# Scores of two heads issued one behind the other on the two halves of the array's rows, and stick-breaking sums in two fp32r passes over split data

## The chip, the core and the metric

The kernel runs on one core of a Trainium2 chip. The metric is the device time of one execution in microseconds (us); the time given for a kernel is the median of its runs.

The core's engines work side by side and meet through semaphores: TensorE (PE, with its weight loads, PEld), VectorE (DVE), ScalarE (ACT), GpSimd (POOL) and SyncE (SP), whose queue starts nearly all transfers from HBM. Each engine takes its own instructions in the order in which they stand. Matmuls read SBUF and write PSUM banks.

## The reference

Two blocks on a sequence of 256 tokens of width 1024, batch 1, all in float32. The first block is a Fourier and convolution mixer and a windowed attention, each followed by a mixture of 16 experts. The second has two layers of: half a feed-forward, three attention branches merged by gates, half a feed-forward. The change touches the windowed attention of the first block and two branches of the second. Of these the stick-breaking branch matters most:

```python
def stick_breaking_attention(q, k, v):          # 8 heads of 64
    ...
        z = jnp.einsum('bqhd,bkhd->bhqk', qb, k).astype(jnp.float32) * scale
        strict = kpos[None, :] < qpos[:, None]
        log_one_minus = jnp.where(strict, -jax.nn.softplus(z), 0.0)
        suffix = lax.cumsum(log_one_minus, axis=3, reverse=True) - log_one_minus
        w = jnp.where(strict, jnp.exp(jax.nn.log_sigmoid(z) + suffix), 0.0)
        return jnp.einsum('bhqk,bkhd->bqhd', w.astype(v.dtype), v)
```

So each head needs scores, then a softplus of them, then a running sum of the softplus along the keys, an exponential, and a product with v. The sparse branch (`nsa_attention`) has 8 heads in 2 groups with a compressed, a selected and a windowed part, each a masked softmax; the latent branch (`mla_attention`) has 8 heads with an ordinary causal softmax. The result of each branch goes through a projection and is multiplied by a sigmoid gate:

```python
        y = (gates[:, :, 0] * (o_sb @ proj_sb[l])
             + gates[:, :, 1] * (o_mla @ proj_mla[l])
             + gates[:, :, 2] * (o_nsa @ proj_nsa[l]))
```

## The kernel before

The 256 tokens are two tiles of 128 rows. Large products are done with split operands: a float32 tile w is cast to fp32r by ACT (`wh`, L289) and the remainder is taken by DVE (`wl`, L290); the product is then three fp32r matmuls, hh with wh, hl with wh and hh with wl (L1197 to L1199). Products of the attention itself are plain fp32 matmuls, which the profile shows as two records each.

The kernel is written for a tile framework. It places instructions on the engines by a list of its own: priority goes by the order in which the program is written, an instruction is taken when the framework's own clock says that its inputs are there, and buffers come from tagged pools. PSUM has the pools `mm` (3 banks, for the large products), `at` (2 banks, for scores), `tr` (2, for transposes) and `oa` (1, for outputs). So the order on PE is a mixture: the steps of an attention head, and between them matmuls of whatever later product has its inputs and a bank. In the second block's attention these are the gate product `gates(0)` on the normalised input (`mm<-hh`, `mm<-hl`) and, once a branch's output is there, its projection (`mm<-oh`, `mm<-ol`).

`attention2` issues, per layer: the input products, the stick-breaking branch (`att_sb`, L1454), the compression of the sparse branch, the latent branch (`att_ml`), the gate product, the projection, and the sparse branch (`att_ns`, L1752). In the profiled execution stick-breaking lies at about 1504 to 1565 us (layer 1) and 2189 to 2249 (layer 2), sparse attention at about 1620 to 1673 and 2304 to 2357.

In `att_sb` a head is 64 wide, so two heads share the 128 partitions of a tile: head 2c has rows 0 to 63, head 2c+1 rows 64 to 127. Four pairs c run one after the other. For a pair the scores of both heads are written to two `at` banks (L1462: 256 and 128 columns per head). Then per head: Abs, Exp and Ln on ACT (L1467 to L1469), the softplus `sp` on DVE (L1471, tile `cpT`), two masks on POOL (L1474), the sums as two fp32 matmuls with a triangle of -1 and a block of -1 into the same bank (L1475, 384 columns; L1476, 128 columns), the Exp of the result on ACT (L1479, the tile w, called `ce`), two masks on POOL (L1482), and the product with v (L1436, L1438) into the `oa` bank. A table load on ACT (ACT_TABLE_LOAD) stands where a function is not in the loaded set; Ln, Exp and the Tanh of the gates (L1397) are such functions. The scores of the next pair wait only for their bank, which the Exp of w sets free.

In `att_ns` the scores of two heads on the two halves of the rows are written by L1770 (128 and 256 columns per head), followed by two mask matmuls, a softmax in `causal` (L1290; its maximum of z is L1305), a transpose (L1313) and the product with v (L1782). In the windowed attention `scores` (L694) writes four 256-wide score matmuls per group of two heads (L701), and `heads` (L711) does the softmax.

The constants of the second block, `negT` and `negones` among them, come in one tile `c2` by a DMA that POOL starts before the second block.

## Time and profile before

| | us |
|---|---|
| median of 3 runs | 2604.27 (2604.23 to 2607.89) |
| the profiled execution | 2607.32 |
| its span in the profile | 2605.6 |
| PE busy | 2197.9 (84%) |
| DVE busy | 1171.4 (45%) |
| ACT busy | 884.0 (34%) |
| POOL busy | 90.9 (3%) |
| mean DMA rate | 267 GB/s |

The profile is of one execution. A record's start is exact; the end of a matmul is modelled, so the time that a matmul holds PE is read from its start to the next start. An idle time in brackets stands at the instruction that waited, with the one that released it. Up to about 1222 us the kernel is in the first block, with the DMA engines busy for most of the time, except in the windowed attention (about 640 to 757); behind it lies the second block.

### The profile page before, as it was taken

What the parts mean: (1) busy time and instruction counts of PE and PEld (TensorE: products, weight loads), DVE (VectorE), ACT (ScalarE), POOL (GpSimd) and SP (SyncE); (2) the same over time, 40 slices, a digit from 0 to 9 for tenths busy, and PEclk for the clock granted to TensorE, in tenths of its full rate; (3) what the DMA queues carried; (4) which work ended last, traced back from release to release, by engine and by line L of the source; (5) the groups of instructions that cost most, each with busy time, mean ns of one, the idle gap of its engine ahead of it and who ended that gap; (6) DMA issues with size and microseconds to landing.
All of it is one profiled execution on the core that took longest, in us unless ns stands there. A gap on an engine that the chain in (4) does not pass through costs nothing.

```text
span 2605.6 us, 38741 instructions
## 1 busy us (share of the span) xinstructions
PE 2197.9 (84%) x16264; PEld 1611.9 (62%) x16264; DVE 1171.4 (45%) x2258; ACT 884.0 (34%) x1493; POOL 90.9 (3%) x138
## 2 busy tenths in 40 slices
PE   6977665656977665656999999999999999999999
PEld 4543111113543111113999878799999997879997
DVE  3452110103661101102656657776565556677664
ACT  4331000002441000001544565554444446655443
POOL 1100000000000000000101010000000000000000
PEclk9989878788989878888999999999999999999999
DMA  9779999999759999998455532255555554324553
GB/s 396 321 323 426 428 427 426 427 427 425 296 199 407 427 427 427 427 427 361 176 178 190 178 130 98 84 185 186 179 186 186 178 172 172 114 82 146 180 192 114
DMA packets 67038, 698.82 MB, mean 268 GB/s; under 512 B 7872, under 2 KB 8768, under 8 KB 14256
## 3 DMA queue, kind: packets, MB, share of 16 engines
q1 hardware_dynamic: 66464, 695.38, 67.5%
q8 instruction: 127, 2.08, 0.3%
q0 software_dynamic: 400, 0.98, 0.2%
q14 instruction: 47, 0.39, 0.0%
HBM read 695.28 MB, written 1.05 MB: 267 GB/s over the span
## 4 chain that ended last, share of the span: by engine, by line
PE 50%; ACT 1%; DVE 1%; issue 0%; POOL 0%; ACTq 0%; DVEq 0%
PE mm L1199 11%; PE mm L1198 11%; PE mm L1197 11%; PE mm L1153 1%; PE mm L1154 1%; PE mm L1155 1%; PE at L1770 1%; PE at L1197 1%; PE at L1199 1%; PE at L1198 1%; PE tr L1313 1%; PE oa L1782 1%; PE oa L1436 1%; ACT wh L289 1%; PE at L1475 0%
## 5 line engine op out<-in xcount | busy, mean ns | idle before, releaser
L290 DVE TENSOR_TENSOR wl<-w,wh 128x1024 fp32r<-128x1024 f32 (+3 forms) x494 | 551.5, 1118 | 405.2 <-ACT wh L289 375.9
L289 ACT CAST wh<-w 128x1024 fp32r<-128x1024 f32 (+3 forms) x494 | 472.7, 959 | 597.7 <-PE mm L1198 416.9
L903 PE MATMUL mm<-w,xg 128*32 128x512 f32 x2048 | 322.7, 756 | 210.5 <-DMA w<-in_moe_w_gate_up_dram 209.0
L1198 PE MATMUL mm<-hl,wh 128*128 128x256 f32 x1728 | 490.7, 284 | 2.5 <-DVE hl L1045 2.5
L1199 PE MATMUL mm<-hh,wl 128*128 128x256 f32 x1728 | 491.2, 284 | 0.0
L1197 PE MATMUL mm<-hh,wh 128*128 128x256 f32 x1728 | 491.2, 284 | 0.0
L903 PEld LDWEIGHTS mm<-w,xg 128*32 128x32 f32 x2048 | 65.0, 124 | 436.0 <-DMA w<-in_moe_w_gate_up_dram 321.4
L1198 PEld LDWEIGHTS mm<-hl,wh 128*128 128x128 f32 x1728 | 326.9, 189 | 4.4 <-DVE hl L1045 3.1
L1199 PEld LDWEIGHTS mm<-hh,wl 128*128 128x128 f32 x1728 | 326.7, 189 | 3.7 <-issue 3.4
L1197 PEld LDWEIGHTS mm<-hh,wh 128*128 128x128 f32 x1728 | 326.7, 189 | 0.6 <-issue 0.3
L923 ACT ACTIVATE sil<-mm 128x256 f32<-128x256 f32 x32 | 12.3, 384 | 766.1 <-PE mm L903 766.1
L940 PE MATMUL at<-w,hidT 128*32 128x256 f32 x2048 | 168.7, 485 | 84.7 <-DMA w<-in_moe_w_down_dram 76.9
L924 DVE TENSOR_TENSOR hid<-mm,sil 128x256 f32<-128x256 f32 x32 | 13.6, 425 | 474.1 <-ACT sil L923 474.1
L940 PEld LDWEIGHTS at<-w,hidT 128*32 128x32 f32 x2048 | 78.3, 134 | 163.9 <-DMA w<-in_moe_w_down_dram 73.9
L948 DVE TENSOR_TENSOR xh<-at,agm 32x256 f32<-32x256 f32 x128 | 53.8, 420 | 272.8 <-PE at L940 271.3
L1198 PE MATMUL mm<-gl,wh 128*128 128x256 f32 x528 | 149.3, 283 | 0.0
L1199 PE MATMUL mm<-gh,wl 128*128 128x256 f32 x528 | 148.8, 282 | 0.0
L1197 PE MATMUL mm<-gh,wh 128*128 128x256 f32 x528 | 148.4, 281 | 0.0
L1197 PEld LDWEIGHTS mm<-gh,wh 128*128 128x128 f32 x528 | 99.8, 189 | 0.0
L1199 PEld LDWEIGHTS mm<-gh,wl 128*128 128x128 f32 x528 | 99.6, 189 | 0.0
L1198 PEld LDWEIGHTS mm<-gl,wh 128*128 128x128 f32 x528 | 98.9, 187 | 0.0
L376 PE MATMUL oa<-w,condp 128*32 128x512 f32 x384 | 56.1, 653 | 13.0 <-DMA w<-in_ada_w_dram 12.2
(571 smaller groups left out, 3343.8 us busy)
## 6 DMA issues: line engine op xcount, KB each, us to landing
w<-in_moe_w_gate_up_dram SPq DMA_DIRECT2D x128, 2048.0 KB, 39.1
w<-in_moe_w_down_dram SPq DMA_DIRECT2D x62, 2048.0 KB, 39.1
w<-in_ffn_wi_dram SPq DMA_DIRECT2D x88, 1024.0 KB, 4.8
w<-in_ada_w_dram SPq DMA_DIRECT2D x24, 2048.0 KB, 15.8
w<-in_w_in_dram SPq DMA_DIRECT2D x40, 1024.0 KB, 4.8
w<-in_ffn_wo_dram SPq DMA_DIRECT2D x35, 1024.0 KB, 4.8
w<-in_ffn_wo_dram SPq DMA_DIRECT2D x12, 768.0 KB, 4.4
w<-in_w_out_dram SPq DMA_DIRECT2D x8, 1024.0 KB, 4.8
```

Of the source, the lines that this page charges most:

```text
L289: self.nc.scalar.copy(wh, w)
L290: self.nc.vector.tensor_sub(wl, w, wh.bitcast(F32))
L376: ins = nc.tensor.matmul(ps[32 * j:32 * j + 32, :], self.condp[:, k, 3 - row:35 - row], w[:, k, :], start=first and r == 0, stop=last and ...
L903: nc.tensor.matmul(ps[32 * j:32 * j + 32], xg[:, k, e * CAP:(e + 1) * CAP], w[:, :, kk, j * 256:(j + 1) * 256], start=k == 0, stop=k == KC ...
L940: nc.tensor.matmul(psd[32 * j:32 * j + 32, :], hT2[:, k % 2, 32 * (k // 2):32 * (k // 2) + 32], w[:, kk, j * 256:(j + 1) * 256], start=k = ...
L948: nc.vector.tensor_tensor(dst, psd[32 * j:32 * j + 32, :], gate[32 * j:32 * j + 32, :], op=ALU.mult)
L1153: nc.tensor.matmul(ps[t], xh[:, k, sl], wh[:, c, :], start=k == 0, stop=False)
L1154: nc.tensor.matmul(ps[t], xl[:, k, sl], wh[:, c, :], start=False, stop=False)
L1155: nc.tensor.matmul(ps[t], xh[:, k, sl], wl[:, c, :], start=False, stop=k == kc - 1)
L1197: nc.tensor.matmul(o, wh[:, cs], xh[:, k, :], start=k == 0 and j == 0, stop=False, skip_group_check=True)
L1198: nc.tensor.matmul(o, wh[:, cs], xl[:, k, :], start=False, stop=False, skip_group_check=True)
L1199: nc.tensor.matmul(o, wl[:, cs], xh[:, k, :], start=False, stop=k == kc - 1 and j == 1, skip_group_check=True)
```

## The change

Four things change.

1. In all three places the score matmuls of the two heads get an edge (`queue_behind`) that orders them on PE behind an earlier instruction, without a semaphore: in the windowed attention behind the last step that used the pair of banks (`bank_exp`), in stick-breaking behind the last POOL mask of w of the pair before (`prev`), in sparse attention behind the last maximum of z (`last_exp`). Both heads' scores thus become ready together for the framework's list.
2. The stick-breaking sums: `sp` is split, `sh` by a cast on ACT and `sl` by a subtraction on DVE, and the two fp32 matmuls become four fp32r ones.
3. The constant matrices are copied once to fp32r (`negr`) by two POOL copies.
4. The scratch memory for DMA descriptors made on the core is set to 2048.

```diff
@@ scores(gp, r, bank), windowed attention
-                        nc.tensor.matmul(sps[g][:, t, :], qT[rs, 4 * gp + r, t * P:(t + 1) * P], kT[rs, gp, :],
-                                         start=t == 0, stop=False)
+                        m = nc.tensor.matmul(sps[g][:, t, :], qT[rs, 4 * gp + r, t * P:(t + 1) * P], kT[rs, gp, :],
+                                             start=t == 0, stop=False)
+                        self.queue_behind(m, self.bank_exp.get(bank))
...
-                nc.vector.tensor_tensor(z, z, es, op=ALU.add)
+                self.bank_exp[bank] = nc.vector.tensor_tensor(z, z, es, op=ALU.add)
...
+    def queue_behind(self, ins, prev):
+
+        if prev is not None:
+            self.tc.add_manual_dep(ins.ins, prev.ins.name,
+                                   mybir.DependencyInfo(mybir.DependencyClass.NoSync, mybir.DependencyReason.DATA),
+                                   reason="pair of row tiles")
...
@@ causal
-        nc.vector.tensor_scalar(z, z, 1e-30, None, op0=ALU.max)
+        self.last_exp = nc.vector.tensor_scalar(z, z, 1e-30, None, op0=ALU.max)
...
@@ att_sb
+                prev = None
                 for c in range(4):
...
-                            nc.tensor.matmul(o, SB.kT[r, c, k0:k0 + P], SB.qT[r, c, k0:S], start=k0 == 0, stop=k0 > 0)
+                            m = nc.tensor.matmul(o, SB.kT[r, c, k0:k0 + P], SB.qT[r, c, k0:S], start=k0 == 0, stop=k0 > 0)
+                            self.queue_behind(m, prev)
...
-                        nc.tensor.matmul(z, self.negT, sp, start=False, stop=False, skip_group_check=True)
-                        nc.tensor.matmul(z[:, P:S], self.negones, sp[:, S:S + P], start=False, stop=True,
-                                         skip_group_check=True)
+
+                        sh = self.T(p, [P, 384], "cmh", 2, F32R)
+                        sl = self.T(p, [P, 384], "cml", 2, F32R)
+                        nc.scalar.copy(sh, sp)
+                        nc.vector.tensor_sub(sl, sp, sh.bitcast(F32))
+                        for s_ in (sh, sl):
+                            nc.tensor.matmul(z, self.negr[:, 0:P], s_, start=False, stop=False, skip_group_check=True)
+                            nc.tensor.matmul(z[:, P:S], self.negr[:, P:2 * P], s_[:, S:S + P], start=False,
+                                             stop=s_ is sl, skip_group_check=True)
...
-                            nc.gpsimd.affine_select(s_, s_, [[1, P]], ALU.is_gt, 0.0, 0, -1)
+                            prev = nc.gpsimd.affine_select(s_, s_, [[1, P]], ALU.is_gt, 0.0, 0, -1)
...
@@ att_ns
+                self.last_exp = None
...
-                                    nc.tensor.matmul(sp[g][:, q0:q0 + k1], NS.qT[gs, r, q0:q1], NS.kT[gs, i, 0:k1],
-                                                     start=q0 == 0, stop=False)
+                                    m = nc.tensor.matmul(sp[g][:, q0:q0 + k1], NS.qT[gs, r, q0:q1], NS.kT[gs, i, 0:k1],
+                                                         start=q0 == 0, stop=False)
+                                    self.queue_behind(m, self.last_exp)
...
@@ second_block
+            self.negr = self.T(self.hp, [P, 2 * P], "negr", 1, F32R)
+            nc.gpsimd.tensor_copy(self.negr[:, 0:P], self.negT)
+            nc.gpsimd.tensor_copy(self.negr[:, P:2 * P], self.negones)
...
@@ kernel
-    nc = bacc.Bacc("TRN2", target_bir_lowering=False, num_devices=1)
+    nc = bacc.Bacc("TRN2", target_bir_lowering=False, num_devices=1, dynamic_dma_scratch_size=2048)
```

How this moves work is seen in the order of the instructions on each engine. Line numbers of the kernel after are higher by 10 to 20: its scores are L1473 (stick-breaking) and L1789 (sparse), its sums L1493 and L1494, its casts and subtractions L1490 and L1491, its products with v L1446, L1448 and L1802, its fp32r products L1200 to L1202, its Abs, Exp and Ln L1479 to L1481, its Exp of w L1497.

First, ACT at heads 7 and 8 of layer 1's stick-breaking branch, before. The banks of the two heads are `at_8960` and `at_8961`; L289 are weight casts, L1397 the Tanh of the gates:

```order
L1479 ACT_TABLE_LOAD
L1479 ACTIVATE ce_8976<-at_8960 128x384
L1467 ACTIVATE ce_8980<-at_8961 128x384
L289 CAST wh_9786<-w_9756 128x1024
L1468 ACTIVATE ce_8980<-ce_8980 128x384
L1469 ACT_TABLE_LOAD
L1469 ACTIVATE ce_8980<-ce_8980 128x384
L289 CAST wh_9820<-w_9818 128x1024
L1397 ACT_TABLE_LOAD
L1397 ACTIVATE mg_9530<-mg_9530 128x512
L1479 ACTIVATE ce_8990<-at_8961 128x384
```

And the same heads on ACT after, in the banks `at_8999` and `at_9000`:

```order
L1481 ACT_TABLE_LOAD
L1481 ACTIVATE ce_9005<-ce_9005 128x384
L1490 CAST cmh_9013<-cpT_9009 128x384
L1497 ACT_TABLE_LOAD
L1497 ACTIVATE ce_9021<-at_8999 128x384
L1479 ACTIVATE ce_9025<-at_9000 128x384
L1480 ACTIVATE ce_9025<-ce_9025 128x384
L1481 ACT_TABLE_LOAD
L1481 ACTIVATE ce_9025<-ce_9025 128x384
L1490 CAST cmh_9033<-cpT_9029 128x384
L1497 ACT_TABLE_LOAD
L1497 ACTIVATE ce_9041<-at_9000 128x384
```

The casts have come in, the weight casts and the Tanh have moved ahead of this place, and table loads now stand at Ln and at the Exp of w of both heads.

Second, PE at the same heads before, behind the sums of head 7 (L1475, L1476 on `at_8960`); L1323 and L1324 are the first scores of the latent branch, L1293 and L1294 its masks, and 25 fp32r matmuls stand between this piece and the sums of head 8:

```order
L1475 MATMUL at_8960<-cpT_8970,c_1034_5850 128x384
L1476 MATMUL at_8960<-cpT_8970,c_1034_5850 128x128
L1199 MATMUL mm_9532<-hh_7345,wl_9594 128x256
L1197 MATMUL mm_9532<-hh_7345,wh_9593 128x256
L1198 MATMUL mm_9532<-hl_7346,wh_9593 128x256
L1199 MATMUL mm_9532<-hh_7345,wl_9594 128x256
L1197 MATMUL mm_9531<-hh_7345,wh_9621 128x256
L1323 MATMUL at_9138<-mqk_9136 128x128
L1436 MATMUL oa_8994<-ce_8976,v_8315 64x256
L1324 MATMUL at_9138<-mqk_9136 128x256
```

And after, from the last sum of head 7 to the first product with v of head 8:

```order
L1494 MATMUL at_8999<-cml_9014,negr_5852 128x128
L1333 MATMUL at_9189<-mqk_9187 128x128
L1446 MATMUL oa_9045<-ce_9021,v_8318 64x256
L1334 MATMUL at_9189<-mqk_9187 128x256
L1303 LDWEIGHTS mskb_1667
L1303 MATMUL at_9189<-mskb_1667 128x128
L1304 LDWEIGHTS mskb_1667
L1304 MATMUL at_9189<-mskb_1667 128x128
L1493 MATMUL at_9000<-cmh_9033,negr_5852 128x384
L1494 MATMUL at_9000<-cmh_9033,negr_5852 128x128
L1493 MATMUL at_9000<-cml_9034,negr_5852 128x384
L1494 MATMUL at_9000<-cml_9034,negr_5852 128x128
```

No fp32r product stands between the two heads' sums any more; 18 of them stand ahead of head 7's sums, where 28 stood before.

Third, PE at the scores of one group of sparse attention in layer 1, before (`at_10439` is the bank of one head, the other head's scores follow further down, behind its masks and fp32r products):

```order
L1197 MATMUL mm_10737<-hh_7345,wh_10741 128x256
L1770 MATMUL at_10439<-nkT_9745,qT_9732 128x128
L1770 MATMUL at_10439<-nkT_9745,qT_9732 128x256
L1293 LDWEIGHTS mskb_1667
L1293 MATMUL at_10439<-mskb_1667 128x128
L1294 LDWEIGHTS mskb_1667
L1294 MATMUL at_10439<-mskb_1667 128x128
L1198 MATMUL mm_10737<-hl_7346,wh_10741 128x256
```

And a group after:

```order
L1789 MATMUL at_10439<-nkT_9796,qT_9783 128x128
L1789 MATMUL at_10440<-nkT_9796,qT_9783 128x128
L1789 MATMUL at_10439<-nkT_9796,qT_9783 128x256
L1802 MATMUL oa_10209<-cpT_10398,nkv_8619 64x256
L1802 MATMUL oa_10209<-cpT_10348,nkv_8619 64x128
L1323 MATMUL tr_10416<-cst_72,ce_10407 128x128 x3
L1802 MATMUL oa_10209<-cpT_10398,nkv_8619 64x128
L1802 MATMUL oa_10209<-cpT_10370,nkv_8619 64x256
L1789 MATMUL at_10440<-nkT_9796,qT_9783 128x256
```

The 128-wide scores of the two heads now stand next to each other; between the 256-wide ones other work of the branch has been put.

## Rows read from the trace of the kernel before

**Rows 1.** The page: PE's busy share in forty slices of the span, in tenths.

```profile
PE   6977665656977665656999999999999999999999
```

**Rows 2.** Stretches: us; PE, PEld, DVE, ACT, POOL busy; granted PE clock; DMA share; GB/s.

```profile
640.00:757.00 117.00, 114.01 (x634) 71.98 (x633) 76.74 (x198) 53.93 (x142) 3.12 (x3) 1.00 0.68 266
...
1504.00:1565.00 61.00, 57.85 (x370) 44.88 (x368) 32.63 (x90) 42.89 (x74) 10.05 (x33) 0.97 0.34 121
...
1620.00:1673.00 53.00, 52.91 (x369) 39.29 (x369) 41.00 (x159) 26.92 (x80) 0.00 (x0) 1.00 0.23 81
...
2189.00:2249.00 60.00, 56.88 (x372) 43.62 (x370) 32.84 (x90) 43.16 (x76) 10.43 (x34) 1.00 0.35 123
```

**Rows 3.** Timeline of PE: start, us, engine, line, out<-in, shape; fp32r fill.

```profile
1505.78 0.28 PE L1197 MATMUL mm<-hh,wh 128*128 128x256 f32 x1
1505.90 0.28 PE L1198 MATMUL mm<-hl,wh 128*128 128x256 f32 x1
```

**Rows 4.** Timeline of PE: scores in windowed (L701) and sparse attention (L1770), first mask.

```profile
668.87 0.70 PE L701 MATMUL at<-kT,xn 64*128 64x256 f32 x4
...
674.64 1.13 PE L701 MATMUL at<-kT,xn 64*128 64x256 f32 x4
...
1635.06 0.92 PE L1770 MATMUL at<-nkT,qT 64*128 64x128 f32 x4
1635.91 0.23 PE L1293 MATMUL at<-mskb 128*128 128x128 bf16 x1
```

**Rows 5.** Timeline of PE: the sums of head 7, layer 1, and what follows.

```profile
1552.38 0.91 PE L1475 MATMUL at<-cpT,c 128*128 128x384 f32 x2 [0.72 <-POOL cpT L1474]
1553.13 0.38 PE L1476 MATMUL at<-cpT,c 128*128 128x128 f32 x2
1553.27 0.36 PE L1199 MATMUL mm<-hh,wl 128*128 128x256 f32 x1
```

**Rows 6.** Waits of PE from 1504 to 1565: total us, times, longest.

```profile
PE at L1323 <- ACT ce L1479: 1.3, 1, 1.3
PE at L1475 <- POOL cpT L1474: 0.9, 2, 0.7
```

**Rows 7.** Timeline of ACT at heads 7 and 8 of layer 1.

```profile
1553.60 1.28 ACT L1479 ACT_TABLE_LOAD   x1 [2.47 <-PE at L1476]
1554.89 0.49 ACT L1479 ACTIVATE ce<-at 128x384 f32<-128x384 f32 x1
1555.28 0.48 ACT L1467 ACTIVATE ce<-at 128x384 f32<-128x384 f32 x1
1555.65 1.05 ACT L289 CAST wh<-w 128x1024 fp32r<-128x1024 f32 x1
1556.58 0.54 ACT L1468 ACTIVATE ce<-ce 128x384 f32<-128x384 f32 x1
1557.13 1.28 ACT L1469 ACT_TABLE_LOAD   x1
1558.43 0.52 ACT L1469 ACTIVATE ce<-ce 128x384 f32<-128x384 f32 x1
```

**Rows 8.** Timeline of POOL at the same heads: masks of sp (L1474) and w (L1482).

```profile
1550.71 1.62 POOL L1474 TENSOR_SCALAR_AFFINE_SELECT cpT<-cpT 128x128 f32<-128x128 f32 x2 [4.93 <-DVE cpT L1471]
1555.45 0.54 POOL L1482 TENSOR_SCALAR_AFFINE_SELECT ce<-ce 128x128 f32<-128x128 f32 x2 [3.12 <-ACT ce L1479]
1559.68 0.54 POOL L1474 TENSOR_SCALAR_AFFINE_SELECT cpT<-cpT 128x128 f32<-128x128 f32 x2 [3.70 <-DVE cnb L1299]
```

**Rows 9.** Groups from 1504 to 1565: a cast (ACT) and subtractions (DVE); busy us, mean ns.

```profile
L1287 ACT CAST oh<-oa 128x256 fp32r<-128x256 f32 x3 | 1.1, 370 | 1.9 <-PE oa L1438 1.9
...
L290 DVE TENSOR_TENSOR wl<-w,wh 128x1024 fp32r<-128x1024 f32 x9 | 11.0, 1221 | 3.8 <-ACT wh L289 2.4 <-PE mm L1199 1.3
L1288 DVE TENSOR_TENSOR ol<-oa,oh 128x256 fp32r<-128x256 f32 x3 | 1.3, 425 | 3.6 <-ACT oh L1287 3.5
```

**Rows 10.** Stretch with a lower granted clock, columns as in rows 2.

```profile
1558.00:1561.00 3.00, 3.00 (x17) 3.00 (x16) 2.26 (x4) 0.94 (x2) 0.54 (x2) 0.55 0.31 57
```

More of the change, by code (lines that the diff above doesn't have):

```diff
@@ L706, in scores, with heads @@
                 return sps
-            def heads(gp, r, sps):
+            self.bank_exp = {}
+            def heads(gp, r, sps, bank):
                 h0 = 8 * gp + r
@@ L762, in windowed @@
                     next(q1, None)
-                heads(0, r, sc)
+                heads(0, r, sc, self.at)
                 if r < 3:
@@ L770, in windowed @@
                 nx = scores(1, r + 1, self.mm if r % 2 == 0 else self.at) if r < 3 else None
-                heads(1, r, sc)
+                heads(1, r, sc, self.mm if r % 2 else self.at)
                 sc = nx
```

## The prediction

> **What bounds the kernel now.** I read the page's slices first, then the table by stage, then the lines and waits of TensorE (PE), and last the timelines of ScalarE (ACT) and GpSimd (POOL). In the page's line of forty slices PE stands at 9 from about the twentieth on [rows 1]. So in the second block, time is PE work plus PE's idle time, and no other engine counts unless PE waits for it. The table by stage says the same where the change lies: of 53.0 us of sparse attention in layer 1 PE is busy 52.9; of 61.0 us of stick-breaking it is busy 57.9 in layer 1, and 56.9 of 60.0 in layer 2 [rows 2]. The windowed stage of the first block is PE-bound too (114.0 of 117.0 us) [rows 2], though what surrounds it there is not. The idle 3.1 us of a stick-breaking stretch have names: 1.3 us for the Exp of w and 0.9 us for the POOL selects [rows 6]; the rest is a copy behind a table load.
>
> PE keeps busy there because the scheduler fills between the heads' steps with split-precision fp32r matmuls of the gate projection, each 256 columns wide and 0.12 us behind the one before (1505.78, 1505.90) [rows 3]. A head's own steps are a long chain on other engines; the fill is what hides it. That is the view to keep in mind below: the change makes PE's part shorter and the chain longer.
>
> **The change part by part: the PE stream.** *Scores.* Two heads whose row tiles stand next to each other run together: four records take 0.70 us paired and 1.13 us unpaired in the windowed stage [rows 4], so a full pair of 256-wide ones saves 0.43 us and a 128-wide one beside a wider one about half, 0.22. Sparse attention has no pair before: one head's four records hold PE 0.85 us (1635.06 to 1635.91) [rows 4]. The order shows how many become neighbours per layer: in sparse attention 5 pairs of 128, 1 of 256 and 2 mixed, of 16 possible, because transposes and output products are put between the others; in stick-breaking 3 mixed ones beyond those that stood together before. That is 5 x 0.22 + 0.43 + 2 x 0.22 + 3 x 0.22 = 2.6 us per layer. In the windowed stage 12 pairs stand together for 10, 2 x 0.43 = 0.85 us once.
>
> *Sums.* A head's two fp32 sums hold PE 0.89 us, from 1552.38 to 1553.27 [rows 5]. After, there are four fp32r matmuls, two of 384 and two of 128 columns. By the 256-wide step [rows 3] a 384-wide one is an estimated 0.18 us. No 128-wide fp32r stands in the trace: its price lies between half of the 256-wide step, 0.06, and the 0.22 that the 128-wide fp32 sum holds PE: 0.14 to the next start (1553.13 to 1553.27) and the 0.08 by which that next one is longer [rows 3, 5]; I take the whole 256-wide step, 0.12, as nearest in form. Then 2 x 0.18 + 2 x 0.12 + 0.1 for entering = 0.70, a gain of 0.19 a head, 1.5 us per layer (0 to 2.5).
>
> *Switches.* The first fp32r matmul after an fp32 one takes 0.36 instead of 0.28 us (1553.27 against 1505.78) [rows 3, 5], so a change of form costs about 0.09. Counted in the two orders, the attention stretch of a layer has 286 changes of form before and 266 after, so 1.8 us less. The Trainium skill ("TensorEngine Tiling (Array Packing)", Key Properties) says that changing the tiling mode drains TensorE; it would speak against more row-tile groups, and the 0.09 is what rows show of it. Since groups become fewer it counts for the change here.
>
> Stream: -2.6 - 1.5 - 1.8 = -5.9 us per layer (-3.5 to -7.5).
>
> **The chain.** Per head the change adds an ACT cast and a VectorE (DVE) subtraction between the POOL selects and the sums. Casts of 256 and 1024 columns take 0.37 and 1.05 us, subtractions 0.43 and 1.22 [rows 7, 9]; for 384 that is by the line 0.48 and 0.56. And the scores of the next pair now stand behind the last POOL select of this pair, where before each head's scores went out as its bank came free. ACT's order, shown above, adds a second thing: per layer 12 instead of 8 table loads in the stretch, since Ln and Exp of the last heads now each have their own. A load holds ACT 1.30 us (1557.13 to 1558.43) [rows 7]. The Trainium skill ("ScalarE: Activation LUTs", What ACT_TABLE_LOAD costs) puts 1.28 us plus a drain of 1.38 on each switch; the rows show no such drain, as the load starts when the Exp ahead of it ends. By the skill's price four loads of the last pair would cost some 5 us more per layer than I count.
>
> The last pair (heads 7 and 8 of a layer) in after's order, from the end of its scores, by rows [rows 7 to 9]: Abs 0.37, Exp 0.55, load 1.30, from Ln's start to the end of the selects 1.79 (1558.43 to 1560.22), cast 0.48, subtraction 0.56, sums of the low half 0.4, load 1.29 (it waits for the sums, as at 1553.60), Exp of w 0.39: 7.1 us. Head 8's Abs stands behind that Exp on ACT, so head 8 goes through the same again, and ends with 1.10 from Exp's start to the selects' end (1554.89 to 1555.99) instead of 0.39: 7.8 us. Together 15.0. In that time PE has in its order 18 fp32r matmuls (2.2 us), the sums (1.4) and one score group of the next branch with its output products (some 1.3): 4.9. PE then sits idle **10 us**, where before 28, 5 and 25 fp32r matmuls stood at these places and 2.2 us were waited for [rows 6]. The fill has been used up: it was put between the earlier heads, and what remains of it needs this branch's output.
>
> The third pair has 74 fp32r matmuls (8.9 us), sums and small work, 11.8 us in all, against a chain of the same 15 to 16 us: 4 us idle at most. Pairs one and two have 72 and 82 of them and the fp32 compression matmuls, 13 to 14 us against 13 to 16. Since fill and chain are near each other there I take 3 us for the three together, not the 6 of the upper ends. So 13.0 instead of 3.1 idle: **+9.9 us per layer** (+4 to +14).
>
> *Clock.* After the wait at 1553.60 the granted clock stood at 0.55 in 1558 to 1561, near the lower of the two levels; 17 matmuls took 3.0 us where 17 x 0.12 = 2.0 would do [rows 10]. Layer 2's stretch has no such clock (1.00) [rows 2]. With longer waits I count one more, +1.0 (0 to 3).
>
> *The rest costs nothing.* The two POOL copies of the constants run in the norm ahead of the second block's first matmuls, where POOL is idle. The smaller DMA scratch leaves the 460 instructions of SyncE's queue and POOL's DMAs in the same order; if it did delay a POOL DMA, the transfers of the first block are bound by weights, not by it. In sparse attention the edge puts scores behind an earlier head's z maximum on DVE. No head there has a table load, a cast or a POOL select in its chain, PE waits 0.1 us in 53 now [rows 2], and fill from the projections still stands between the heads; if that cover went, eight groups with 0.5 us each would cost 4 us a layer, which the range holds.
>
> **The sum.** Per layer -5.9 + 9.9 = +4.0; two layers +8.0; windowed -0.85; clock +1.0: +8.2 us. On the profiled execution (2607.3 us, of it 2605.6 span) this gives 2615.5. That execution was 3.0 above the median of 2604.3, which I take as spread between runs, so 2612.5, rounded **2612**.
>
> **The rivals.** *The fill still hides the chain* (faster). Then idle time stays at 3.1 us and the stream's gain comes through: 2 x -5.9 - 0.85 = -12.7, 2591.6. For it: PE's fill of pairs one to three is hardly smaller than before, and the casts are short. Against it: 18 matmuls stand before the last pair's sums and none between head 7's and head 8's. It decides where idle time grows by under 3.7 us a layer, since -5.9 + 3.7 doubled is -4.4, with the windowed stage -5.2. Chance 0.14. *Both cancel*: the last pair idles 7 us instead of 10 and the others stay covered, +6 against -5.9: 2604, chance 0.23. *The pairs do not run together*: the two halves share more than the windowed stage shows, the scores' 2.6 and 0.85 are lost: 8.2 + 6.05 = +14.2, 2618, chance 0.05. *Everything small is dear*: 128-wide fp32r at 0.22, selects at the 1.6 us seen once, idle +13, a half-clock stretch in each layer: 2 x (-4.5 + 13) - 0.85 + 3 = +19, 2623, chance 0.08. The forecast, 2606 to 2618, has 0.50.
>
> **How the numbers follow.** A measurement of this kernel can tell 0.2%, 5.2 us, from no change: 2599.1 to 2609.5 counts as same. Slower: 0.43 of the forecast's 0.50, and 0.13 of the last two, 0.56, and 0.02 from the upper edge of the cancelling case: 0.58. Same: 0.07 of the forecast, 0.17 of the cancelling case, 0.02 of the first rival: 0.26. Faster: 0.12 of the first rival and 0.04 of the cancelling case's lower edge: 0.16. The range 2596 to 2624 leaves out most of the first rival and a little above the last.
>
> **What would show it.** In the profile of after: idle time of PE in each stick-breaking stretch (57.9 of 61.0 now) grows to about 13 us, most of it at the sums and output products of heads 7 and 8, waiting for casts, subtractions and the Exp of w behind table loads; 12 table loads there; sums of 0.70 us a head; pairs of scores that start together; sparse attention shorter by 1 to 3 us with no wait; perhaps stretches of clock near 0.5. The prediction is wrong if PE's idle time there stays under 7 us, if the sums' fp32r passes cost as fp32, or if time moves in a stage that is not attention.

## The result: 30 us slower, where 8 were forecast

The changed kernel takes 2635.9 us (median of 4 runs, 2633.5 to 2637.8) against 2606.1 for the kernel before in the same runs (2604.2 to 2608.0): a ratio of 1.0115, 95% interval 1.0099 to 1.0131. The forecast was 2612, in a range of 2596 to 2624. The sign was right; the size was not.

The span grew from 2605.6 to 2633.6 us, by 28.0. From the first starts of the scores' lines in the two traces: the windowed attention takes 6.6 us of it (the first stick-breaking scores start at 1510.9 for 1504.3), layer 1 takes 9.8 (from one layer's first scores to the next layer's 694.8 for 685.0), and layer 2 the last 11.6. No other stage moved by more than 0.3 us.

These are the stretches of the changed kernel, columns as in [rows 2]: the windowed stage, stick-breaking in layer 1, sparse attention in layer 1, stick-breaking in layer 2, and the last pair of heads of layer 1 by itself. The first line is of the kernel before, for the windowed stage.

```profile
669.00:735.00 66.00, 63.01 (x396) 34.44 (x396) 45.13 (x134) 30.79 (x102) 2.08 (x2) 1.00 0.65 251
669.00:742.00 73.00, 68.45 (x403) 35.04 (x401) 45.18 (x134) 30.81 (x102) 2.08 (x2) 0.95 0.63 243
1511.00:1582.00 71.00, 60.55 (x405) 48.43 (x405) 37.78 (x101) 54.24 (x92) 10.86 (x34) 0.92 0.34 119
1641.00:1700.00 59.00, 57.13 (x408) 41.87 (x408) 44.53 (x149) 30.23 (x80) 0.00 (x0) 1.00 0.22 76
2206.00:2277.00 71.00, 60.18 (x406) 48.02 (x405) 37.99 (x102) 54.17 (x92) 10.85 (x34) 0.93 0.33 119
1568.00:1584.00 16.00, 9.73 (x34) 6.34 (x33) 4.23 (x12) 9.49 (x17) 2.15 (x8) 0.58 0.00 0
```

Two columns matter. PE idles 10.5 us of a stick-breaking stretch (71.00 less 60.55), where [rows 2] had 3.1. And the granted clock is 0.92 and 0.93 over a whole stretch, 0.58 in the last pair, where before one stretch of layer 1 alone was low [rows 10]. The waits of PE from 1511 to 1582 answer to [rows 6] (total us, times, longest):

```profile
PE at L1493 <- ACT cmh L1490: 5.6, 4, 2.3
PE oa L1446 <- POOL ce L1500: 2.6, 4, 0.9
PE tr L1677 <- issue: 0.9, 1, 0.9
PE at L1333 <- ACT ce L1497: 0.6, 1, 0.6
```

The sums wait for the new cast, the output products for the masks of w, and a score for the Exp of w. The chain that the prediction walked through shows on ACT (timeline, answering to [rows 7]) at heads 7 and 8:

```profile
1565.98 0.49 ACT L1479 ACTIVATE ce<-at 128x384 f32<-128x384 f32 x1 [0.33 <-PE at L1473]
1566.51 0.53 ACT L1480 ACTIVATE ce<-ce 128x384 f32<-128x384 f32 x1
1567.05 1.28 ACT L1481 ACT_TABLE_LOAD   x1
1568.34 0.52 ACT L1481 ACTIVATE ce<-ce 128x384 f32<-128x384 f32 x1
1570.09 0.51 ACT L1490 CAST cmh<-cpT 128x384 fp32r<-128x384 f32 x1 [1.23 <-POOL cpT L1486]
1570.62 1.28 ACT L1497 ACT_TABLE_LOAD   x1
1572.08 0.49 ACT L1497 ACTIVATE ce<-at 128x384 f32<-128x384 f32 x1 [0.18 <-PE at L1494]
1572.47 0.48 ACT L1479 ACTIVATE ce<-at 128x384 f32<-128x384 f32 x1
...
1577.26 0.51 ACT L1490 CAST cmh<-cpT 128x384 fp32r<-128x384 f32 x1 [1.92 <-DVE cnb L1309]
1577.79 1.28 ACT L1497 ACT_TABLE_LOAD   x1
1579.25 0.49 ACT L1497 ACTIVATE ce<-at 128x384 f32<-128x384 f32 x1 [0.18 <-PE at L1494]
```

From Abs of head 7 at 1565.98 to the output product of head 8 at 1580.15 are 14.2 us; the walk had 15.0. (The load for the Exp of w starts ahead of the sums here, not behind them as at 1553.60 in [rows 7], which saves time; the sums, at half the clock, take some of it back.) On PE the same time looks like this; the waits stand in brackets:

```profile
1567.86 0.28 PE L1200 MATMUL mm<-oh,wh 128*128 128x256 f32 x1
...
1570.66 0.68 PE L1493 MATMUL at<-cmh,negr 128*128 128x384 f32 x1 [2.29 <-ACT cmh L1490]
1571.13 0.31 PE L1494 MATMUL at<-cmh,negr 128*128 128x128 f32 x1
...
1572.62 0.79 PE L1333 MATMUL at<-mqk 96*128 96x128 f32 x2 [0.58 <-ACT ce L1497]
...
1577.82 0.69 PE L1493 MATMUL at<-cmh,negr 128*128 128x384 f32 x1 [1.99 <-ACT cmh L1490]
...
1580.15 0.69 PE L1446 MATMUL oa<-ce,v 128*64 128x256 f32 x1 [0.94 <-POOL ce L1500]
```

Also to be seen: the 384-wide sum lasts 0.68 us here, and 0.34 to 0.45 in the heads before, at full clock. From 1570.7, just behind the wait of 2.29 us, the granted clock was at half, and the little work that PE had ran at half speed. PE idles 5.8 us of these 14.2, where the walk had 10 of 15.

### The profile page after: what moved, and what is told of

It is laid out like the page before. It is cut to its first block, busy times and chain, and to the rows that moved or that the text cites. A ratio compares the mean times of both kernels' runs of the same rounds, so it can differ in the third digit from the quotient of the medians.

```text
span 2633.6 us, 38778 instructions
## 1 busy us (share of the span) xinstructions
PE 2200.0 (84%) x16264; PEld 1606.9 (61%) x16264; DVE 1182.9 (45%) x2274; ACT 902.1 (34%) x1517; POOL 91.3 (3%) x140
## 4 chain that ended last, share of the span: by engine, by line
PE 48%; ACT 2%; DVE 2%; issue 1%; POOL 0%; ACTq 0%; DVEq 0%; POOLq 0%
PE mm L1201 11%; PE mm L1200 11%; PE mm L1202 11%; PE mm L1156 1%; PE mm L1158 1%; PE mm L1157 1%; DVE wl L290 1%; PE at L1200 1%; PE at L1789 1%; PE at L1201 1%; PE at L1202 1%; PE tr L1323 1%; PE oa L1802 1%; PE oa L1446 1%; ACT wh L289 1%
## 5 line engine op out<-in xcount | busy, mean ns | idle before, releaser
L289 ACT CAST wh<-w 128x1024 fp32r<-128x1024 f32 (+3 forms) x494 | 472.6, 959 | 581.7 <-PE mm L1201 402.3
L1200 PE MATMUL mm<-hh,wh 128*128 128x256 f32 x1728 | 490.9, 284 | 0.0
L1202 PE MATMUL mm<-hh,wl 128*128 128x256 f32 x1728 | 489.3, 283 | 0.0
L1200 PEld LDWEIGHTS mm<-hh,wh 128*128 128x128 f32 x1728 | 325.9, 189 | 4.4 <-issue 4.1
L1202 PEld LDWEIGHTS mm<-hh,wl 128*128 128x128 f32 x1728 | 326.0, 189 | 1.3 <-issue 1.1
L927 DVE TENSOR_TENSOR hid<-mm,sil 128x256 f32<-128x256 f32 x32 | 13.6, 424 | 490.1 <-ACT sil L926 490.1
L943 PE MATMUL at<-w,hidT 128*32 128x256 f32 x2048 | 163.4, 473 | 78.0 <-DMA w<-in_moe_w_down_dram 69.2
L1202 PE MATMUL mm<-gh,wl 128*128 128x256 f32 x528 | 148.8, 282 | 0.0
L1200 PE MATMUL mm<-gh,wh 128*128 128x256 f32 x528 | 148.5, 281 | 0.0
L1200 PEld LDWEIGHTS mm<-gh,wh 128*128 128x128 f32 x528 | 99.9, 189 | 0.0
L1202 PEld LDWEIGHTS mm<-gh,wl 128*128 128x128 f32 x528 | 99.5, 189 | 0.0
L376 PE MATMUL oa<-w,condp 128*32 128x512 f32 x384 | 58.6, 665 | 13.0 <-DMA w<-in_ada_w_dram 12.0
```

The source lines that it names most:

```text
L289: self.nc.scalar.copy(wh, w)
L376: ins = nc.tensor.matmul(ps[32 * j:32 * j + 32, :], self.condp[:, k, 3 - row:35 - row], w[:, k, :], start=first and r == 0, stop=last and ...
L943: nc.tensor.matmul(psd[32 * j:32 * j + 32, :], hT2[:, k % 2, 32 * (k // 2):32 * (k // 2) + 32], w[:, kk, j * 256:(j + 1) * 256], start=k = ...
L1200: nc.tensor.matmul(o, wh[:, cs], xh[:, k, :], start=k == 0 and j == 0, stop=False, skip_group_check=True)
L1202: nc.tensor.matmul(o, wl[:, cs], xh[:, k, :], start=False, stop=k == kc - 1 and j == 1, skip_group_check=True)
```

## Where the layers' time went, by line

Since every matmul's start is exact, the time from each start to the next, less idle time, can be added up by line. This was done for layer 2, from its first scores to the first matmul of the feed-forward behind the attention. This is the hold of a line; the hold of all lines together is the stream. The three kernels beside before are experiments told of below, chosen because their clock stood at 1.00 throughout layer 2; the changed kernel itself is told of behind the table. All are us, and the last row also holds smaller lines that the table leaves out.

| layer 2 | before | windowed and sparse edge, split sums (e5) | no edge, split sums, other gates (e8) | e8 and the sparse edge (e10) |
|---|---|---|---|---|
| fp32r products | 146.0 | 144.4 | 146.4 | 144.1 |
| stick-breaking sums | 7.5 | 5.1 | 4.6 | 4.6 |
| stick-breaking scores | 7.2 | 7.2 | 7.2 | 7.2 |
| sparse scores | 13.6 | 12.2 | 13.6 | 10.4 |
| transposes (L1313) | 7.1 | 9.8 | 7.3 | 9.0 |
| masks on scores | 2.5 | 3.0 | 2.5 | 2.9 |
| products with v | 20.3 | 21.2 | 20.7 | 20.8 |
| PE idle | 3.7 | 8.3 | 2.2 | 2.4 |
| layer's attention | 229.3 | 232.1 | 225.5 | 222.3 |

For the changed kernel itself the same sums give: idle 13.5 (layer 1: 13.2 for 3.9), hold of all lines 227.4 for 225.7. Its granted clock was at the lower level for 13.7 us of layer 2, in which PE was busy for 10.0. If that work takes half the time at the full clock, 5.0 us of the hold are the clock's, and the stream at full clock is 227.4 - 5.0 = 222.4, that is 3.3 less than before. The kernel of e5, with the same orders but for stick-breaking's scores and its clock at 1.00, bears this out: without those scores its lines hold PE 5.3 us less than those of the changed kernel. Layer 2 is then +9.9 idle, +5.0 clock, -3.3 stream, together +11.6. In layer 1, where before had a stretch of 3.4 us at the lower level (1.7 us) and after 13.7 with 9.7 busy (4.8), it is +9.3 idle, +3.1 clock, -2.6 stream, together +9.8.

Idle time and clock are not independent in this account. Where PE waits for a chain on other engines, its own work at half the clock can fill time in which it would have idled. So the clock's share is an account of the hold; no run shows what the two layers would take with these waits at full clock.

## Experiments

Where no number of runs is given, a time is of one execution. Executions of one kernel differ: the kernel before took from 2604.4 to 2613.0 us beside e1. The attention of a layer, from its first scores to the feed-forward behind it, repeats to 0.2 us where two kernels share it (e3 and the changed kernel, e10 and e11), so single executions are best compared by it. A low stretch is one with the granted clock at the lower level, 0.50 of full speed.

Theory A: the ordering edges are the cause. They put a pair's scores behind the end of the pair before, so that the chains of two pairs no longer overlap, and the fill runs out before the last pair. Theory B: the split's cast and subtraction, and the table loads that come with the new order on ACT, make each chain too long to be hidden, edge or not.

**e1: no edges, split sums kept.**

```diff
-                            self.queue_behind(m, prev)
+                            pass
```

and the same at the other two places.

> The kernel after, with none of the three ordering edges on the scores; the two fp32r passes over split sums and the rest stay. Theory A (the edges put a pair's scores behind the end of the pair before, so the chains of two pairs no longer overlap and PE starves): the time falls to 2600 to 2610 us, PE idle in each stick-breaking stretch back to 3 to 6 us, the windowed stage back to its old length. Theory B (the longer chain with cast and subtraction is what starves PE): it stays at 2620 to 2630, with only the windowed stage's 6.5 us given back.

Measured: 2611.8 us (10 runs) against 2606.5, a ratio of 1.0019 (1.0009 to 1.0029). Of the 30 us, 24 go with the edges. Up to layer 1 nothing was lost (its first scores at 1504.3, as before). But this is a little above the bound that theory A gave, and idle time is 6.8 us in a layer's attention, 6.3 of them up to the end of the latent branch, not 3 to 6: the split sums without edges cost some 5 us, though their PE work is cheaper. (The scratch and the two copies of the constants, which e1 and e3 keep, cost nothing that shows: the first scores of layer 1 start at 1504.3 and 1504.4, for 1504.3 before.) The waits from 1504 to 1580:

```profile
PE at L1493 <- ACT cmh L1490: 2.4, 2, 1.3
PE oa L1446 <- POOL ce L1500: 1.5, 2, 1.1
PE tr L1677 <- issue: 0.9, 1, 0.9
```

The sums still wait for the cast, half as long as in the changed kernel. So theory A holds for most of the loss, theory B for a rest.

**e2: all three edges, sums as two fp32 matmuls.** The cast and the subtraction go with the split.

```diff
-                        for s_ in (sh, sl):
-                            nc.tensor.matmul(z, self.negr[:, 0:P], s_, start=False, stop=False, skip_group_check=True)
...
+                        nc.tensor.matmul(z, self.negT, sp, start=False, stop=False, skip_group_check=True)
```

> The kernel after, with the sums as two fp32 matmuls as before; the three edges stay. Theory A (edges): about as slow as after, 2630 to 2642, since the sums get dearer again by some 2.7 us a layer while the chain loses about 1.1 us per head. Theory B (split chain): the time falls to 2608 to 2618, the windowed stage's 6.5 us staying.

Measured: 2626.1 us, between the ranges of the two. Idle time is 11.2 us in both layers, so the edges by themselves bring 7.3 to 7.6 of the 9.3 to 9.9; the split adds 2 on top of them and 3 without them. What the split adds most is the clock: with fp32 sums the low stretches of the two layers are 3.4 and 0 us long, with split sums 13.7 each.

**e3: no edge in the windowed attention.**

> The kernel after without the edge in the windowed attention alone. If that edge moved the scores behind the matmuls that wait for weights and brought on the half-clock stretch there, 6 to 7 us go and the rest stays: 2627 to 2631, second block's stages as after. If the shift comes from elsewhere (the DMA scratch, say), nothing goes: 2634 to 2638.

Measured: 2629.2 us, and both layers' attention within 0.1 us of the changed kernel's. So this edge alone carries the 6.6 us, and they reach the end undiminished, although a stage with the DMA engines busy for 96% of the time (740 to 1222 us before) lies between. What happened there shows on PE of the changed kernel from 703 to 714 us:

```profile
705.25 1.05 PE L394 MATMUL oa<-cst,arow 128*128 128x4 f32 x8 [0.75 <-ACT arow L391]
706.57 0.55 PE L408 MATMUL oa<-rw,acol 128*1 128x16 f32 x16 [0.27 <-DVE acol L395]
707.96 0.60 PE L412 MATMUL oa<-rbr,cst 1*128 1x16 f32 x2 [0.83 <-DVE rbr L410]
708.83 3.62 PE L376 MATMUL oa<-w,condp 128*32 128x512 f32 x10 [0.27 <-DVE rbl L414]
```

and in its stretches, whose granted clock is the third figure from the end:

```profile
708.00:710.00 2.00, 1.73 (x10) 0.83 (x11) 1.33 (x7) 0.00 (x0) 0.00 (x0) 0.50 1.03 442
710.00:712.00 2.00, 2.00 (x6) 0.18 (x1) 0.23 (x1) 0.00 (x0) 0.00 (x0) 0.50 1.00 426
```

In the kernel before, transposes, products and the scores of two groups stood between these small steps of the conditioning (L394, L408, L412), a chain over DVE and ACT. From L408 to L412 it is the scores:

```profile
709.07 0.55 PE L408 MATMUL oa<-rw,acol 128*1 128x16 f32 x16
709.55 1.13 PE L701 MATMUL at<-kT,xn 64*128 64x256 f32 x8
...
710.95 1.13 PE L701 MATMUL mm<-kT,xn 64*128 64x256 f32 x8
...
712.34 0.39 PE L412 MATMUL oa<-rbr,cst 1*128 1x16 f32 x2
```

With the edge those scores come later, and the chain stands bare. From the first windowed score to the last output product the stage takes 95.1 us for 88.8, and three parts account for it. PE idles 4.6 us for 3.0. The clock costs 2.9, half of the 5.7 us of work in the low stretch from 707 to 714 us. The stream at full clock grows by 1.9: the transposes hold PE 9.2 us for 8.3, the products with v 12.1 for 11.4, the conditioning's products (L376) 13.6 for 13.0, and the scores 12.8 for 12.6, although four more pairs of their records start together (22 for 18), while the fp32r products give some 0.6 back.

Idle time and stream repeat in all five kernels here with this edge (4.5 to 4.6 idle, 87.7 to 87.8 stream) and in all eight without it (3.0, and 85.6 to 85.9). The low stretch does not: it lasted 3.4 or 6.8 us with the edge and none or 3.4 without. So some 3.4 of the 6.6 us come with the edge in every execution, and the clock's part here is at the upper end of what the executions show.

**e4: the gates' Tanh replaced by a scaled copy.** This kernel leaves out the sigmoid of the gates.

```diff
-                        nc.scalar.activation(gb, gb, AF.Tanh, scale=0.5)
+                        nc.scalar.activation(gb, gb, AF.Copy, scale=0.5)
```

> The kernel after with the gates' Tanh replaced by a plain scaled copy on ScalarE, so the gates are left out of the computation and no table load stands between Ln and Exp any more (15 loads in all for 37). The order changes with it. If the table loads of Ln and Exp are half of the last pair's chain, as the walk had it (four of 1.29 us out of 15), PE idle in each stick-breaking stretch falls by 5 to 8 us and the time to 2612 to 2624; if serial dependence alone starves PE, idle falls by less than 3 us a layer and the time stays above 2628.

Measured: 2622.6 us, in the range of the first case. But idle time falls to 9.5 us in layer 1 and 9.6 in layer 2, by some 4 and not by 5 to 8; the low stretches fall to 6.8 and 10.2 us. Table loads are a good part of the chain, but without any of them in it 5.6 and 5.9 us of idle time a layer stay over before.

**e5 and e6: one edge less, in stick-breaking and in sparse attention.** The edits are as in e1, at one place each.

> The kernel after without the edge in stick-breaking alone; the edges in the windowed and the sparse attention and the split sums stay. If the stick-breaking edge carries the loss in the second block, the two layers come to what they are without any edge (+2 us each over before) and the windowed stage keeps its +6.5: 2616 to 2620. If the sparse attention's edge carries it (1.9 us of idle PE in that stretch, and fill that is taken from elsewhere), a layer stays 5 us or more over before: 2623 to 2634.

> The kernel after without the edge in the sparse attention alone. Should the sparse attention's edge gain (pairs together), the time rises to 2638 or more; should its 1.9 us of idle PE outweigh the pairs, it falls to 2630 to 2634; a fall below 2626 would say that it, not the stick-breaking edge, carries the loss.

Measured: 2618.3 and 2631.4 us. Without the stick-breaking edge the layers take 233.3 and 232.1 us, for 240.5 and 241.0 in the changed kernel and 232.0 and 231.9 in e1, without any edge: of the two edges in the second block the stick-breaking one carries the loss. e6 is 4.4 us below the changed kernel, inside the range of its second case, but its two layers take 240.6 and 239.4 us for 240.5 and 241.0; 2.7 us of the fall lie ahead of the second block, where the executions differ (the low stretch of the windowed stage was half as long in this one). So the sparse edge moves the changed kernel's layers by 1.6 us at most. The e5 column of the table shows why it does not gain there: 14 pairs of the scores' records start together (none before) and the scores give back 1.4 us, but transposes, masks and products with v, which now stand singly between row tiles, take 4.1 more, and the fp32r products 1.6 less. What a transpose costs by its neighbour shows in the kernel before (L1313 is the transpose, L1770 a score on one half of the rows):

```profile
1652.32 0.27 PE L1313 MATMUL tr<-cst,ce 128*128 128x128 f32 x1
1652.35 0.36 PE L1199 MATMUL mm<-oh,wl 128*128 128x256 f32 x1
1652.56 0.38 PE L1313 MATMUL tr<-cst,ce 128*128 128x128 f32 x2
1652.87 0.92 PE L1770 MATMUL at<-nkT,qT 64*128 64x128 f32 x4
```

A transpose holds PE 0.03 us ahead of an fp32r product, which in turn holds it 0.2 instead of 0.12, and two transposes ahead of a score hold it 0.31, 0.11 for the first and 0.20 for the second.

**e7: the kernel before with the gates by Exp, Ln and Exp.** The sigmoid is computed as exp(-ln(1 + exp(-x))), from one table.

```diff
-                        nc.scalar.activation(gb, gb, AF.Tanh, scale=0.5)
+                        nc.scalar.activation(gb, gb, AF.Exp, scale=-1.0)
+                        nc.scalar.activation(gb, gb, AF.Ln, bias=1.0)
+                        nc.scalar.activation(gb, gb, AF.Exp, scale=-1.0)
...
-                            nc.vector.scalar_tensor_tensor(yb, gb, 1.0, ps, op0=ALU.add, op1=ALU.mult)
+                            nc.vector.scalar_tensor_tensor(yb, gb, 2.0, ps, op0=ALU.mult, op1=ALU.mult)
```

> The kernel before, with the gates' sigmoid made of Exp, Ln and Exp instead of Tanh: two more ACT passes for each gate tile, but no change of table (15 loads in all for 29). If table loads in the heads' chain are what PE waits for in the kernel before (3.1 us idle a layer and a half-clock stretch of 1 us or more behind it), the time falls by 3 to 8 us, to 2598 to 2603; if the added ACT work lengthens the chain as much, it stays within 3 us of before.

Measured: 2606.4 us (10 runs), a ratio of 1.0001 (0.9992 to 1.0010): no change, so the hoped-for gain did not come. The low stretch of layer 1 is as long as before and only stands later (at 1623 us, behind the latent branch, for 1557), and PE still idles 3.4 us in a layer up to the end of the latent branch (3.8 and 3.6 before). The wait moved:

```profile
PE at L1477 <- POOL cpT L1476: 1.3, 2, 1.1
PE tr L1661 <- issue: 0.9, 1, 0.9
```

It is now the sums that wait for the POOL masks. With fewer loads the order gives PE less fill between the heads (17 fp32r products before head 6's sums for 29, 16 before head 8's for 30). That the cover shrank with the chain is a reading of the order; no run shows it apart.

**e8: e7's gates, split sums, no edge.**

> No edges, split fp32r sums, and the gates by Exp, Ln and Exp. If the split sums lose without edges only because their longer chain stands behind table loads, PE idle in stick-breaking falls from 6.3 to about 2 us a layer, the half-clock stretch goes, and the stream's gain of some 2.7 us a layer comes through: 2594 to 2601, below the previous run and below before. If cast and subtraction alone make the chain too long, it stays above 2606.

Measured: 2598.5 us (6 runs), a ratio of 0.9973 (0.9960 to 0.9986). Idle time is 2.1 and 2.2 us a layer, the clock 1.00:

```profile
1504.00:1565.00 61.00, 59.48 (x415) 47.95 (x414) 41.02 (x109) 44.66 (x91) 10.79 (x34) 1.00 0.37 124
2184.00:2245.00 61.00, 59.47 (x415) 48.06 (x414) 41.00 (x109) 44.81 (x91) 10.78 (x34) 1.00 0.36 125
```

PE is busy 59.5 of 61 us where [rows 2] had 57.9. Here the sums' gain of 2.9 us a layer (4.6 for 7.5 in the table) comes through. Neither half of it gains alone: e1 is slower than before, e7 equal to it.

**e9 and e10: e8 with one edge put back.**

> The version without edges and with gates by Exp, Ln and Exp, with the stick-breaking edge put back alone. There is no table load between Ln and Exp here. If the edge starves PE by itself, since a pair's scores stand behind the end of the pair before and the fill is used up ahead of the last pair, idle PE in stick-breaking rises from 1.9 to 6 us or more a layer, and the time from 2598.5 to 2606 to 2614. If the edge only hurts together with table loads, it stays below 2602.

> The same version with the sparse attention's edge put back alone. Scores should hold PE 1.4 us a layer less (14 neighbouring starts for none). If that comes back at the transposes, masks and output products that now stand singly between row tiles (some 4 us more hold in the kernel after), and with 1.5 us of idle PE, the time rises by 2 to 6 us to 2600 to 2605; if the pairs are a gain by themselves, it falls to 2594 to 2597.

Measured: 2614.4 and 2593.5 us. With the stick-breaking edge, idle time goes from 2.2 to 7.2 us in each layer, and low stretches of 7 and 10 us come back, with no table load in any chain:

```profile
PE at L1495 <- ACT cmh L1492: 2.8, 2, 2.0
PE oa L1448 <- POOL ce L1502: 1.8, 3, 0.9
```

So this edge starves PE by itself. It costs 5.2 and 6.0 us in the layers, 11.1 of the 15.9 us between the two times; the rest lies ahead of the windowed attention, where the two kernels do not differ (its first score starts at 672.5 for 667.6 us). The sparse edge did better than either of the expectations, with 6.2 us less in the two layers. In layer 2, 3.2 us of the scores' hold go (19 pairs of records start together, 14 in e5) and only 2.3 come back at transposes, masks and products with v, while the fp32r products lose 2.4; half of that is that fewer of them follow another form (60 for 74, each at 0.20 us for 0.12). Idle time stays at 2.4.

**e11: e10 again, in five runs.**

> The previous kernel again (split sums, the edge in sparse attention alone, gates by Exp, Ln and Exp), timed in rounds. If its one time was no accident, the median is 2592 to 2596, 0.4 to 0.55% under before, with the interval below 1; if it was, it is that of the version without the edge, 2598.

Measured: 2591.9 us (5 runs) against 2608.2, a ratio of 0.9941 (0.9928 to 0.9955), just below the range given for no accident. This version, with the split sums, the edge in sparse attention alone and the gates by Exp, Ln and Exp, is faster than both kernels: by 0.6% than the one before, by 1.7% than the change as it was made.

## The prediction, point by point

**What bounds.** Right: the time followed PE's hold and PE's idle time, and these two account for the 28.0 us of the two layers and the windowed stage to within 0.3.

**The idle time of PE (+9.9 a layer).** Measured +9.3 and +9.9 over the whole attention of layers 1 and 2, but this agreement is in part luck. Up to the end of the latent branch it is +7.5 and +8.0, at the places and for the releasers named: sums behind the cast, output products behind the masks, Exp of w behind its load. The other 1.9 us lie in sparse attention, which was forecast to have no wait:

```profile
1647.85 0.36 PE L1200 MATMUL mm<-oh,wh 128*128 128x256 f32 x1 [1.72 <-DVE cz L1318]
```

There an fp32r product waits for the normaliser of a head on DVE. The walk along the order with durations of [rows 7 to 9] gave the last pair's chain to 0.8 us in 15. The idle time in it was 5.8 us and not 10, since PE's own work there took 8.4 us and not 4.9, most of it at half the clock. That the stick-breaking edge is the main cause (e1, e5, e9) and the table loads and the split a second one (e4, e8) is shown.

**The sums (-1.5 a layer).** Measured -2.4 to -2.9 at full clock (e5, e8). The unknown price was at the cheap end: a 128-wide fp32r matmul holds PE for 0.06 us from start to start, half of the 256-wide step and not all of it, where another fp32r matmul or a transpose follows. The last sum of a head in e8 and the matmul behind it (timeline of PE):

```profile
1512.08 0.22 PE L1496 MATMUL at<-cml,negr 128*128 128x128 f32 x1
1512.14 0.35 PE L1687 MATMUL tr<-c,chs 128*128 128x30 f32 x2
```

**The scores (-2.6 a layer).** Measured -1.7 in stick-breaking (7.2 to 5.5 in the changed kernel) and -1.4 in sparse attention, -3.1 together in layer 2: about right.

**The switches (-1.8 a layer): the first step that failed.** I took the changes of form, counted them (286 to 266) and gave each the same 0.09 us. Not all have that price. Its row (1553.27, in [rows 5]) is an fp32r product behind a sum on the whole array, not behind a row tile, so it does not show what a change of the array's tiling costs. At the fp32r products the gain did come (-1.6 in e5). But the transposes went from 7.1 to 9.8 us there, since a transpose followed by a row tile holds PE 0.20 us and one followed by an fp32r product 0.03 (rows under e6), and the masks and products with v rose by 1.4 more. With sums and scores at -5.5, the rest of the stream is some +2.2 in layer 2 where -1.8 was forecast: this term had the wrong sign, and the stream came to -2.6 and -3.3 a layer instead of -5.9.

**The clock (+1.0 in all): the second.** I counted one more short stretch like that of [rows 10]. With waits of 2 us one behind the other, the granted clock stayed at half, the lower of the two levels, for 13.7 us in each layer. In the account of the hold that is 3.1 us more in layer 1 and 5.0 in layer 2, where I had put down 3 at most in all; how much of it PE would have idled at full clock stays open. (The wait at 1553.60, which the prediction names as the cause before, is one of ACT; PE's own waits there are 0.72 us at 1552.38 and 1.3 for the Exp of w, in [rows 5] and [rows 6].)

**The windowed stage (-0.85): the third, and the largest in one place.** It took +6.6. I counted only pairs of scores there, and did not follow what the edge moves against the conditioning chain on the same engine, although the order shows it. In its place the runs show idle time (+1.6), a low stretch (+2.9) and a stream longer by 1.9 us, at transposes and products; the scores themselves gained nothing. The rule for a moved step, that each queue it is moved past counts, was applied to stick-breaking and not here.

The sum of the misses: 5.9 for the stream (11.8 forecast, 2.6 and 3.3 measured), 7.1 for the clock (8.1 less 1.0), 7.5 for the windowed stage, 0.6 less for the idle time: 19.9, and the 28.0 measured less the 8.2 forecast are 19.8.

**The rivals.** "The fill still hides the chain" did not happen with this change, but does in e8, without the edges and with another gate function, though the cast is there: the cover, not the cast, decides. "Everything small is dear" came nearest in size, for other reasons: the sums were cheap, and clock and windowed stage dear. As to the table load, the rows of the changed kernel show the Ln starting 1.29 us behind the load's start (1567.05 to 1568.34), as before, with no drain of its own.

## What to carry to other kernels

An edge that makes two instructions neighbours also fixes their place in the queue. Ask first which chains overlapped across that place, and whether independent work is left at the last of them. Here a cheaper step on the bound engine gained nothing while its longer chain was not covered (e1), and gained once it was (e8). Lost cover showed up not only as idle time but also as work at half the clock behind the waits. Where forms of matmul alternate, price each neighbourship by its own rows and not by a mean switch.

## What was not expected of the hardware

Two row tiles that are neighbours start 7 ns apart, but one output product between them undoes it: in sparse attention's split groups a 256-wide score that stands alone holds PE 0.63 us in its two records, where it held 0.53 behind the 128-wide one in the kernel before. And the half-clock stretches did not end with the waits: in the last pair of layer 1 the clock was at half from about 1571 to 1584 us, with PE busy 9.7 of the 13.7 us, while in the kernel with the same edges and fp32 sums, which idles only 2 us less a layer, it was at half for 3.4 us or not at all.
